# A two-layer decoder trunk: the loads of the modulation weights go from SyncE's DMA queue to GpSimd's, one background step ahead

## The chip, the cores and the metric

One core of one Trainium2 chip. The number that counts is the device time of one execution in microseconds, as the median of several runs.

## What is computed

Two decoder layers on 512 tokens of width 1024, in float32. In each layer the input is normalized and modulated, mixed by attention (a dilated attention with three head groups in layer 0, a forgetting attention in layer 1), added back through a gate, normalized and modulated again, and sent through 16 experts of which each token uses two. The six modulation rows of a layer come from one vector c:

```
ada_in = jax.nn.silu(c)
mod = (ada_in @ w_ada[i] + b_ada[i]).reshape(b, 6, d)
sh_m, sc_m, g_m = mod[:, 0, None, :], mod[:, 1, None, :], mod[:, 2, None, :]
sh_f, sc_f, g_f = mod[:, 3, None, :], mod[:, 4, None, :], mod[:, 5, None, :]
hm = rmsnorm(x, norm_mix[i]) * (1 + sc_m) + sh_m
...
x = x + g_m * y
hf = rmsnorm(x, norm_ffn[i]) * (1 + sc_f) + sh_f
x = x + g_f * hierarchical_moe(hf, ...)
```

Here `w_ada[i]` is 1024 x 6144, so that each of the six rows needs a 1024 x 1024 block of weights, 4 MB.

## The kernel before, in words

Matrix products run on TensorE as three float32r products of a high and a low part (`part`, L289). Weights arrive as tiles of 128 x 1024 floats through `Stream` (L78): `fetch` starts a load on SyncE's queue (L114), and `split` makes the high part on ScalarE (L150) and the low part on VectorE (L151).

The attention of layer 0 (`mixer_a`, L634) runs over four quarters of the heads. In each, a generator of main steps (`project`, L493) does projections, and `weave` (L225) puts steps of the attention of the quarter before between them. In every second main step `weave` also advances the first generator in a list of background jobs by one step. There are ten such jobs (`background`, L322): each makes one modulation row that is needed later, with `ada` (L382). The first two rows of layer 0 were made at the start (`begin`).

A job of `ada` clears an accumulator on GpSimd (L387) and puts the bias row into it (L388, on GpSimd's DMA queue). Then come eight steps, and in each it takes a tile of 512 KB, loads one eighth of the weights into it (L391, on SyncE's queue) and adds that tile, times one column of silu(c), to the accumulator on VectorE (L392, a scalar_tensor_tensor, STT below). In three of the jobs the fifth step also loads a row of norm weights (L394, SyncE's queue). After the eighth step ScalarE makes the high part (L397), VectorE the low part (L398), and three steps later four matmuls with a column of ones add up the partitions (L404, L407). The row is scaled (L411) or copied (L413) and written to memory by ScalarE's queue (L414).

The tiles of the weight stream and of the jobs share one pool tag, "raw", with four buffers. The stream holds at most three of them in this stage (L108), and a job takes one at a time.

The text of the program does not fix the order on an engine. A scheduler in the tile framework orders the instructions of each engine when the kernel is built, by priorities and a model of durations of its own, gives out the buffers and sets the waits. On the chip each engine and each DMA queue then goes through its list in that order, and an instruction that waits holds up all that stand behind it on the same engine.

Of the kernel before, what the change touches and what calls it, by code (L numbers as in the profile page):

```python
# [8 lines left out]
F32 = mybir.dt.float32  # L9
# [8 lines left out]
P = 128  # L18
D = 1024
S = 512  # L20
KT = D // P
# [154 lines left out]
class Trunk:  # L176
# [205 lines left out]
    def ada(self, layer, j, norm, put):  # L382

        nc, i = self.nc, self.i
        acc = self.w.tile([P, D], F32, name="acc", tag="acc", bufs=1)
        row = self.nrow
        nc.gpsimd.memset(acc, 0.0)  # L387
        nc.gpsimd.dma_start(out=acc[0:1, :], in_=i["b_ada"][layer:layer + 1, j * D:(j + 1) * D])  # L388
        for kt in range(KT):
            raw = self.w.tile([P, 1024], F32, name="ada", tag="raw", bufs=4)  # L390
            nc.sync.dma_start(out=raw, in_=i["w_ada"][layer, kt * P:(kt + 1) * P, j * D:(j + 1) * D])  # L391
            nc.vector.scalar_tensor_tensor(acc, raw, self.csil[:, kt:kt + 1], acc, op0=OP.mult, op1=OP.add)  # L392
            if norm is not None and kt == KT // 2:
                nc.sync.dma_start(out=row, in_=self.bcast(norm, D, 1))  # L394
            yield
        hi, lo = self.w.tile([P, 1024], F32R, name="ada", tag="raw", bufs=4), self.nlo
        nc.scalar.activation(hi, acc, AF.Copy)  # L397
        nc.vector.tensor_tensor(lo, acc, hi.bitcast(F32), op=OP.subtract)  # L398
        for _ in range(3):
            yield  # L400
        ts = [self.bank("s")[0:1, :], self.bank("s")[0:1, :]]
        for h in range(2):
            cs = slice(h * 512, (h + 1) * 512)
            nc.tensor.matmul(ts[h], lhsT=self.one, rhs=hi[:, cs], start=True, stop=False)  # L404
        for h in range(2):
            cs = slice(h * 512, (h + 1) * 512)
            nc.tensor.matmul(ts[h], lhsT=self.one, rhs=lo[:, cs], start=False, stop=True)  # L407
        for h in range(2):
            cs = slice(h * 512, (h + 1) * 512)
            if norm is not None:  # L410
                nc.vector.scalar_tensor_tensor(row[:, cs], ts[h], 1.0, row[:, cs], op0=OP.add, op1=OP.mult)  # L411
            else:
                nc.scalar.activation(row[:, cs], ts[h], AF.Copy)  # L413
        nc.scalar.dma_start(out=put, in_=row)  # L414
        if (layer, j) == (0, 2):
            self.g_m = self.load_row(layer, 2)
# [986 lines left out]
```

## Time and profile before

| what | value |
|---|---|
| median of 3 runs | 1437.47 us (1434.62 to 1438.4) |
| the profiled execution | 1427.06 us, span 1425.3 us |
| mean granted TensorE clock | 0.966 |
| PE busy (matmul) | 1311.6 us, 92% |
| DVE busy | 967.4 us, 68% |
| ACT busy | 652.4 us, 46% |
| POOL busy | 121.0 us, 8% |
| SyncE's DMA queue (q1) | 227.86 MB, 48.9% of 16 engines' time |
| GpSimd's DMA queue (q0) | 16.85 MB, 5.0% |

PE is TensorE, DVE VectorE, ACT ScalarE, POOL GpSimd, and SP SyncE, which only starts transfers; SPq is its queue. "Idle before" of a group is the time in which its engine did nothing just ahead of these instructions, with what ended most of it. The jobs of `ada` lie between 50 and 560 us; what the tables call "50 to 560" is this stage.

### The profile page before, as it was taken

Reading aid. Unit: us, or ns where it says so; the run is one execution under the profiler, and the core shown is the slowest. Engines: PE = TensorE matmul, PEld = TensorE weight load, DVE = VectorE, ACT = ScalarE, POOL = GpSimd, SP = SyncE. Lnnn points to the kernel's source line nnn. Section 1 sums busy time; section 2 is a strip of 40 time slices with the busy share of each in tenths; the row PEclk is TensorE's granted clock in tenths of the full one; section 3 lists DMA queues with packets and bytes.
Section 4 is the critical chain, followed back from the end, with each engine's and each line's share of the span. In section 5 each row is a group of like instructions: output and inputs, shape, how many; then the busy total and the mean of one; then the engine's idle time right before and its main releaser. Section 6 shows DMA issues by size and latency. Waiting matters only on the chain. (4 is left out here: it accounts for less than half of the span.)

```text
span 1425.3 us, 20009 instructions
## 1 busy us (share of the span) xinstructions
PE 1311.6 (92%) x7017; PEld 1068.2 (75%) x7017; DVE 967.4 (68%) x1913; ACT 652.4 (46%) x1356; POOL 121.0 (8%) x120
## 2 busy tenths in 40 slices
PE   5899999999998999989979998499999999699995
PEld 4787989888996899878756665268988978566662
DVE  6875776676677676655677775486767854877772
ACT  6433544344435444443355554354554542365560
POOL 0000000000000000000032221000000000223221
PEclk9899999999999999989979999799999999899998
DMA  9465445643554445264789997413321465799981
GB/s 360 138 207 179 153 156 162 202 141 120 169 191 151 161 148 164 82 218 149 254 268 313 294 295 233 148 50 95 112 65 62 134 202 191 258 288 303 302 278 22
DMA packets 187156, 264.14 MB, mean 185 GB/s; under 512 B 23065, under 2 KB 148697, under 8 KB 187047
## 3 DMA queue, kind: packets, MB, share of 16 engines
q1 hardware_dynamic: 160742, 227.86, 48.9%
q0 software_dynamic: 8576, 16.85, 5.0%
q10 hardware_dynamic: 17728, 18.05, 4.3%
q8 instruction: 59, 0.97, 0.3%
q14 instruction: 51, 0.41, 0.1%
HBM read 249.85 MB, written 25.43 MB: 193 GB/s over the span
## 5 line engine op out<-in xcount | busy, mean ns | idle before, releaser
L293 PE MATMUL ps_pj<-hi,h 128*128 128x512 f32 (+1 forms) x1016 | 390.6, 393 | 9.6 <-ACT h L453 5.0
L294 PE MATMUL ps_pj<-lo,h 128*128 128x512 f32 (+1 forms) x1016 | 371.9, 374 | 0.0
L296 PE MATMUL ps_pj<-hi,h 128*128 128x512 f32 (+1 forms) x1016 | 290.0, 374 | 0.0
L293 PEld LDWEIGHTS ps_pj<-hi,h 128*128 128x128 f32 x1016 | 238.6, 235 | 32.7 <-ACT h L453 7.1
L294 PEld LDWEIGHTS ps_pj<-lo,h 128*128 128x128 f32 x1016 | 240.3, 237 | 14.4 <-issue 0.8
L296 PEld LDWEIGHTS ps_pj<-hi,h 128*128 128x128 f32 x1016 | 211.5, 235 | 20.0 <-issue 1.1
L150 ACT ACTIVATE hi<-raw 128x1024 fp32r<-128x1024 f32 x126 | 132.4, 1052 | 130.3 <-PE ps_pj L296 70.7
L151 DVE TENSOR_TENSOR lo<-raw,hi 128x1024 fp32r<-128x1024 f32 x126 | 151.8, 1213 | 48.1 <-ACT hi L150 46.1
L392 DVE SCALAR_TENSOR_TENSOR acc<-ada,csil,acc 128x1024 f32<-128x1024 f32 x80 | 102.6, 1283 | 69.0 <-DMA ada<-in_w_ada 68.8
L293 PE MATMUL ps_pj<-hi,xh 128*112 128x512 f32 x256 | 104.9, 410 | 2.2 <-ACT xh L453 2.2
L294 PE MATMUL ps_pj<-lo,xh 128*112 128x512 f32 x256 | 104.2, 407 | 0.0
L296 PE MATMUL ps_pj<-hi,xl 128*112 128x512 f32 x256 | 80.8, 397 | 0.0
L453 ACT ACTIVATE xh<-ps_t 128x448 fp32r<-128x448 f32 x64 | 31.8, 542 | 81.8 <-PE ps_t L448 75.7
L1235 DVE SCALAR_TENSOR_TENSOR y<-ps_s,r_ws,g_f 112x512 f32<-112x512 f32 x64 | 47.8, 748 | 28.5 <-PE ps_s L1234 28.5
L462 DVE TENSOR_REDUCE qss<-sq 128x8 f32<-128x512 f32 x64 | 43.7, 682 | 31.5 <-ACT sq L460 30.8
L460 ACT ACTIVATE sq<-ps_pj 128x512 f32<-128x512 f32 x63 | 37.1, 589 | 57.7 <-PE ps_pj L296 50.9
L151 DVE TENSOR_TENSOR lo<-h,hi 128x1024 fp32r<-128x1024 f32 x42 | 51.1, 1223 | 15.4 <-ACT hi L150 14.6
L720 PEld LDWEIGHTS ps_o<-vr,pt 128*128 128x128 f32 x480 | 58.6, 193 | 1.4
L720 PE MATMUL ps_o<-vr,pt 128*128 128x64 f32 x480 | 57.8, 272 | 0.0
L293 PEld LDWEIGHTS ps_pj<-hi,xh 128*112 128x112 f32 x256 | 45.5, 178 | 15.4 <-ACT xh L453 3.1
L296 PEld LDWEIGHTS ps_pj<-hi,xl 128*112 128x112 f32 x256 | 44.9, 176 | 15.6 <-DVE xl L454 0.6
L927 ACT ACTIVATE nl<-nl,mn 128x128 f32<-128x128 f32 (+1 forms) x64 | 35.7, 559 | 40.6 <-DVE mn L925 40.1
(280 smaller groups left out, 2176.8 us busy)
## 6 DMA issues: line engine op xcount, KB each, us to landing
ada<-in_w_ada SPq DMA_DIRECT2D x85, 512.0 KB
raw<-in_a_w_in SPq DMA_DIRECT2D x128, 256.0 KB
h<-in_w_gate SPq DMA_DIRECT2D x42, 256.0 KB
h<-in_w_up SPq DMA_DIRECT2D x42, 256.0 KB
mix<-in_w_gate SPq DMA_DIRECT2D x37, 256.0 KB
mix<-in_w_up SPq DMA_DIRECT2D x37, 256.0 KB
raw<-in_w_down SPq DMA_DIRECT2D x18, 512.0 KB
h<-in_w_down SPq DMA_DIRECT2D x18, 512.0 KB
```

What stands on the lines that cost most here:

```text
L150: t.act = nc.scalar.activation(h, r, AF.Copy)
L151: nc.vector.tensor_tensor(l, r, h.bitcast(F32), op=OP.subtract)
L293: nc.tensor.matmul(out, lhsT=hi, rhs=wh, start=first and n == 0, stop=False)
L294: nc.tensor.matmul(out, lhsT=hi, rhs=wl, start=False, stop=False)
L296: nc.tensor.matmul(out, lhsT=lo, rhs=wh, start=False, stop=last and n == len(terms) - 1)
L392: nc.vector.scalar_tensor_tensor(acc, raw, self.csil[:, kt:kt + 1], acc, op0=OP.mult, op1=OP.add)
L453: self.nc.scalar.activation(hv, tv, AF.Copy)
L460: nc.scalar.activation(sq, ps, AF.Square)
L462: nc.vector.tensor_reduce(ss, sq.rearrange("p (h d) -> p h d", d=HD), axis=AX.X, op=OP.add)
L720: nc.tensor.matmul(held["o"][:, at:at + HD], lhsT=pt[:, a * P:(a + 1) * P], rhs=v, start=(m == 0), stop=(m == len(terms) - 1))
L927: nc.scalar.activation(pr[:, sl], pr[:, sl], AF.Exp, scale=-1.0, bias=mn, accum_out=held["d"][:, h * 4 + b:h * 4 + b + 1])
L1235: nc.vector.scalar_tensor_tensor(y[:, cs], yp, m["ws"][0:CAP, e:e + 1], m["g_f"][0:CAP, cs], op0=OP.mult, op1=OP.mult)
```

## The change

The loads of `ada` go to GpSimd's queue, and the load of the next eighth is written directly behind the STT of the one before, with a step of its own for the first load. A job has 13 steps where it had 12 (130 of the 140 that the stage's main steps give). The three norm rows go to ScalarE's queue.

```
         nc.gpsimd.dma_start(out=acc[0:1, :], in_=i["b_ada"][layer:layer + 1, j * D:(j + 1) * D])
+
+        def load(kt):
+            raw = self.w.tile([P, 1024], F32, name="ada", tag="raw", bufs=4)
+            nc.gpsimd.dma_start(out=raw, in_=i["w_ada"][layer, kt * P:(kt + 1) * P, j * D:(j + 1) * D])
+            return raw
+
+        raw = load(0)
+        yield
         for kt in range(KT):
-            raw = self.w.tile([P, 1024], F32, name="ada", tag="raw", bufs=4)
-            nc.sync.dma_start(out=raw, in_=i["w_ada"][layer, kt * P:(kt + 1) * P, j * D:(j + 1) * D])
             nc.vector.scalar_tensor_tensor(acc, raw, self.csil[:, kt:kt + 1], acc, op0=OP.mult, op1=OP.add)
+            if kt + 1 < KT:
+                raw = load(kt + 1)
             if norm is not None and kt == KT // 2:
-                nc.sync.dma_start(out=row, in_=self.bcast(norm, D, 1))
+                nc.scalar.dma_start(out=row, in_=self.bcast(norm, D, 1))
             yield
```

The scheduler answers with another order on every engine in this stage. In the new file lines behind L394 carry a number that is 10 higher (L404 becomes L414), the load L391 is L392 and the STT L392 is L400.

On PE, at the end of the fifth job, before (`ada` is the high part, `nlo` the low part, `qn` a normalized query and key block, `ps_pj` the bank of a projection):

```order
L293 MATMUL ps_pj<-hi,h 128x512
L294 MATMUL ps_pj<-lo,h 128x512
L296 MATMUL ps_pj<-hi,h 128x512 x2
L655 MATMUL ps_t<-J,qn 128x128 [waits DVE_49,Activation_49]
L656 MATMUL ps_t<-ident,qn 128x128
L655 MATMUL ps_t<-J,qn 128x128
L404 MATMUL ps_s<-ada,one 1x512 [waits Activation_49]
L404 MATMUL ps_s<-ada,one 1x512
L656 MATMUL ps_t<-ident,qn 128x128
```

and at the same place of the program after the change:

```order
L665 MATMUL ps_t<-J,qn 128x128
L666 MATMUL ps_t<-ident,qn 128x128
L296 MATMUL ps_pj<-hi,h 128x256 x2
L414 MATMUL ps_s<-ada,one 1x512 [waits DVE_49,PE_49]
L417 MATMUL ps_s<-nlo,one 1x512
L414 MATMUL ps_s<-ada,one 1x512 [waits DVE_49,PE_49]
L417 MATMUL ps_s<-nlo,one 1x512
```

The four matmuls now stand together and later, in the value projection, and the first of them no longer waits for ScalarE.

On SyncE's queue, behind the first quarter's loads of the near attention's result (`op`), before (`raw` are tiles of the weight stream):

```order
L765 DMA op<-near_d 128x264 x2
L391 DMA ada<-in_w_ada 128x1024 x5
L114 DMA raw<-in_a_w_in 128x4x256
L114 DMA raw<-in_a_w_in 128x2x256 x2
L391 DMA ada<-in_w_ada 128x1024
L114 DMA raw<-in_a_w_in 128x2x256 x4
L391 DMA ada<-in_w_ada 128x1024 x2
L394 DMA nrow<-in_norm_ffn 1x1024
L391 DMA ada<-in_w_ada 128x1024
```

and at the same place after:

```order
L775 DMA op<-near_d 128x264 x4
L114 DMA raw<-in_a_w_in 128x2x256 x6
L114 DMA raw<-in_a_w_in 128x4x256 x2
L114 DMA raw<-in_a_w_in 128x2x256 x26
L772 DMA near_d<-ox 128x264 x4
```

No job load stands between the weight loads any more, up to the next quarter's stores of `near_d`. On POOL the job loads now stand between the memsets, the bias rows and the merges of the near attention (L787, now L797); from the fifth job to the seventh:

```order
L387 MEMSET acc 128x1024
L388 DMA acc<-in_b_ada 1x16x64
L392 DMA ada<-in_w_ada 128x1024 x8
L387 MEMSET acc 128x1024
L388 DMA acc<-in_b_ada 1x16x64
L392 DMA ada<-in_w_ada 128x1024 x6
L797 TENSOR_TENSOR op<-op,mg_3656 128x4x256
L392 DMA ada<-in_w_ada 128x1024 x2
```

Before, POOL had no load of weights; now its order decides when these start, and a merge stands between the last two loads of the sixth job and the six ahead of them.

Behind the attention stage of layer 0 the order of the engines is the same as before.

## Rows read from the trace of the kernel before

**Rows 1.** Granted clock and busy time by stretch (busy us, in brackets instructions begun), attention stage of layer 0.
```profile
core 0: us, PE busy (x) PEld busy (x) DVE busy (x) ACT busy (x) POOL busy (x), PEclk, DMA share, GB/s
...
130.00:140.00 10.00, 7.71 (x39) 5.73 (x38) 6.35 (x14) 3.97 (x11) 0.00 (x0) 1.00 0.53 168
...
280.00:290.00 10.00, 5.98 (x24) 3.56 (x23) 7.46 (x19) 4.63 (x13) 0.00 (x0) 0.83 0.47 146
...
430.00:440.00 10.00, 5.83 (x27) 3.56 (x25) 7.55 (x18) 4.58 (x13) 0.00 (x0) 1.00 0.54 174
440.00:450.00 10.00, 9.89 (x56) 7.49 (x57) 5.40 (x14) 4.57 (x15) 1.47 (x2) 0.83 0.25 77
...
sum 510.00, PE 491.84 PEld 445.53 DVE 347.21 ACT 220.81 POOL 18.30; mean PE 9.64 PEld 8.74 DVE 6.81 ACT 4.33 POOL 0.36
```

**Rows 2.** The waits of PE, 50 to 560 us: us in total, times, longest.
```profile
PE ps_s L404 <- ACT ada L397: 10.8, 6, 3.1
...
PE ps_t L700 <- ACT nl L691: 2.4, 3, 0.8
PE ps_t L655 <- DVE qn L468: 1.8, 3, 1.1
PE ps_t L655 <- DVE rs_t L215: 1.6, 1, 1.6
PE ps_s L407 <- DVE nlo L398: 1.2, 3, 0.4
```

**Rows 3.** Timeline, end of the fifth job: start us, us, instruction, [idle before].
```profile
281.35 1.28 DVE L392 SCALAR_TENSOR_TENSOR acc<-ada,csil,acc 128x1024 f32<-128x1024 f32 x1
...
282.66 0.34 SPq L391 DMA_DIRECT2D ada<-in_w_ada  x1
...
286.95 1.28 DVE L392 SCALAR_TENSOR_TENSOR acc<-ada,csil,acc 128x1024 f32<-128x1024 f32 x1 [1.37 <-DMA ada<-in_w_ada]
...
288.27 1.06 ACT L397 ACTIVATE ada<-acc 128x1024 fp32r<-128x1024 f32 x1 [3.52 <-DVE acc L392]
...
289.38 0.63 PE L404 MATMUL ps_s<-ada,one 128*1 128x512 f32 x2 [2.28 <-ACT ada L397]
```

**Rows 4.** Groups of instructions by line, 50 to 560 us.
```profile
L392 DVE SCALAR_TENSOR_TENSOR acc<-ada,csil,acc 128x1024 f32<-128x1024 f32 x80 | 102.6, 1283 | 69.0 <-DMA ada<-in_w_ada 68.8
L151 DVE TENSOR_TENSOR lo<-raw,hi 128x1024 fp32r<-128x1024 f32 x62 | 75.2, 1222 | 17.6 <-ACT hi L150 16.1 <-DMA ada<-in_w_ada 1.0
```

**Rows 5.** The waits of DVE, 50 to 560 us.
```profile
DVE acc L392 <- DMA ada<-in_w_ada: 68.8, 49, 3.8
DVE qss L462 <- ACT sq L460: 24.3, 21, 2.2
DVE lo L151 <- ACT hi L150: 16.1, 19, 1.8
DVE rs_t L215 <- ACT rs_y L214: 14.1, 19, 1.8
```

**Rows 6.** The waits of SyncE's DMA queue, 50 to 560 us.
```profile
SPq L394 <- DMA mods<-nrow: 4.7, 2, 3.7
```

**Rows 7.** Tile ada, all instructions: count, min/median/max ns, first and last start.
```profile
L391 SPq DMA_DIRECT2D ada<-in_w_ada x80: 327/340/393, 52.8 to 539.6; - x80
```

**Rows 8.** GpSimd by line and shape, whole span.
```profile
L1196 POOL DMA_INDIRECT xr<-hf_d,r_ii x32 | 37.7, 1178 | 46.6 <-PE ps_t L448 34.5 <-issue 6.7 <-DVE r_wt L1161 5.1
...
L388 POOL DMA_DIRECT2D acc<-in_b_ada x10 | 5.0, 495 | 2.9 <-POOL acc L387 2.9
```

**Rows 9.** Timeline, POOL and DVE, at the first gathers of layer 0.
```profile
719.52 1.22 DVE L151 TENSOR_TENSOR lo<-mix,hi 128x1024 fp32r<-128x1024 f32 x1
...
719.82 1.84 POOL L1196 DMA_INDIRECT xr<-hf_d,r_ii  x1 [2.53 <-DVE r_wt L1161]
```

**Rows 10.** Timeline, PE, two matmuls in full flow.
```profile
109.94 0.40 PE L294 MATMUL ps_pj<-lo,h 128*128 128x512 f32 x1
110.18 0.40 PE L293 MATMUL ps_pj<-hi,h 128*128 128x512 f32 x1
```

## Prediction

> **What bounds the kernel now.** I read the page first: PE is 92% busy over the span, DVE 68%, POOL 8%. The change touches only the stage from 50 to 560 us, so I cut that stage into pieces of 10 us. It is TensorE's stage: PE is busy 491.84 of 510 us, DVE 347.21, POOL 18.30, and the 18.2 us in which PE did nothing lie in a few pieces, such as 2.3 us at 130 to 140, 4.0 us at 280 to 290 and 4.2 us at 430 to 440 [rows 1]. Two of the pieces have a granted clock of 0.83 in place of 1.00, one of them the slice with the 4.0 us gap, the other right behind the 4.2 us gap [rows 1]. So nothing can be won here beyond some 18 us of waits and about 3.4 us of clock (two times 10 us times 0.17); a faster load that PE never waited for is worth nothing.
>
> Next, who PE waited for. The largest item is L404, the matmul at the end of a background job, with 10.8 us in 6 waits, and L407 behind it with 1.2; the rest is transposes, 2.4, 1.8 and 1.6 us [rows 2]. No wait for weights of the projections is on that list, so that the weight loads on SyncE's queue, though they stand behind job loads, were in time for PE. One such end of a job in the timeline shows the chain [rows 3]: the seventh STT starts at 281.35 and ends some 1.28 us later; the eighth load is issued at 282.66, because its buffer is the one that this STT has just read; its STT starts at 286.95, 4.29 us after the issue; ScalarE's split starts at 288.27, and PE goes on at 289.38 after 2.28 us of nothing. The buffer, not the text of the program, sets when a load starts.
>
> DVE pays more than PE: the 80 STTs waited 68.8 us for their loads, 49 times [rows 4, 5]. DVE is idle 510 - 347.2 = 163 us in the stage, so 94 us of it for other reasons, of which 30 us are round trips through ScalarE (L151 16.1, L215 14.1) [rows 5]. PE felt little of that: its waits behind DVE and ScalarE work other than the job ends are 2.4 + 1.8 + 1.6 = 5.8 us [rows 2], 8% of 68.8.
>
> **The change, part by part.** *The fetch one step ahead.* The order of the built programs says which instruction frees the buffer of each load. I added up the DVE work that stands between that instruction and the STT, with the durations of the line groups (1.28 us for an STT, 1.22 for L151 [rows 4], and so on): 3.2 us on average over the 80 loads before, 3.4 after. The fetch ahead is hardly one: the four shared buffers are still handed on at the last moment. Its worth is about 0.25 us per load, for DVE.
>
> *The place of the final matmuls.* The extra step and the new order move L404 back. For each job I take PE's work from the last point at which DVE had to wait for PE to L404, with 0.24 us per 512-column matmul [rows 10], less DVE's work from the same point through the eighth STT. Before, this margin is 3.2, 2.0, 1.1, 5.1, 2.1, 1.1, 5.1, 2.1, 1.1 and 5.1 us for jobs one to ten: six jobs have 2.1 or less, and there were six waits. After, it is 3.2, 3.8, 4.6, 6.9, 7.4, 8.3, 6.4, 12.5, 9.9 and 4.1: all where no job waited before. I count 10 of the 12 us of L404 and L407 as gained, and 2 as left for jobs one to three and ten, since loads will come later (next item). If the cover is thinner than this, the 12 come back in part.
>
> *The queue.* All 80 loads leave SyncE's queue, where one takes 0.34 us to issue [rows 7]; GpSimd has to make their descriptors. The trace has no load of this shape on POOL. From below: the bias row's DMA takes 0.495 us there; the nearest row in size is the gather of 112 rows, 1.18 us [rows 8]; from above, a gather that started beside a low-part subtraction on DVE, 1.84 us [rows 9]. Against 0.34 that is 0.15, 0.84 or 1.5 us later per load. I take 0.84, for the size. POOL has room: 80 x 1.18 = 94 us on top of 18.3 in 510. Net of the 0.25 the STTs see loads 0.6 us later, 80 x 0.6 = 47 us more for DVE to wait. DVE's other idle time less the round trips, 94 - 30 = 64 us, covers that, but not everywhere: at 8% PE would feel 4 us. I take 5, and keep 0 and 12 (a quarter) as ends.
>
> Of descriptors made by GpSimd the Trainium skill (DMA: Bandwidth & Descriptors, Latency and other measured facts) gives a first byte after about 1 us, against about 0.6 for the hardware queues. By that a load would be 0.4 us later, less than the gather's row says, and the sum would be some 3 us better; no run here shows it yet.
>
> *SyncE's queue* loses 80 loads and the waits for their buffers. PE waited for no weight, so I cost this at nothing; it helps ScalarE and DVE to be early.
>
> *Norm rows.* Each must wait until the row before has been written out; on SyncE that was 4.7 us in 2 waits, up to 3.7 [rows 6]. On ScalarE such a wait holds up the work behind it; ScalarE is busy 221 of 510 us [rows 1]. Between 0 and 4.7, I take 1 us.
>
> *The clock.* The slow pieces lie at the two longest gaps; without them up to 3.4 us come back. The 1.6 us of transposes in the slice at 280 us may stay, so I take 1.5.
>
> Sum: -10 - 1.5 + 5 + 1 = **-5.5 us**. On the profiled execution's 1427.06 us that makes 1421.6; that execution was 10 us faster than the median shown, and I set the same difference against the median: 1437.5 - 5.5 = **1432 us**. A measurement of this kernel can tell about 0.3%, 4.3 us, from no change.
>
> **The rivals.** *A wash.* The loads are bound to their buffers as before, DVE's longer waits give PE some 12 us of new stalls, and the 12 us of the job ends are only half won: -6 - 1.5 + 12 + 1, or with the low end of the queue a little less. It gives 1437 within 4 us. For it: the lead of 3.2 to 3.4 us. Against it: the margins, all above 3, and PE's deafness to DVE's waits so far.
>
> *DVE becomes the bound, and it is slower.* Place: the 80 STTs. If loads come on average 1.2 us later than now, DVE waits 80 x (1.2 - 0.25) = 76 us more against 64 us of cover; 12 us go straight to PE, 5 as above, 1 for the norm rows, and of the job ends' 12 only 6 are won: +12 us, **1450 us**. It decides from about 64 / 80 + 0.25 = 1.05 us on. With 1.5 us for every load it would be 100 - 64 = 36 in place of 12, some 1474. For it: two-input operations on DVE stretched a gather from 1.18 to 1.84 us [rows 9], and this stage is full of them, 142 STTs and subtractions [rows 4]. Against it: the bias DMAs, also plain copies, took 0.495 us on average in the same stage [rows 8], and a plain load need not read a tile of indices as the gather does. This is a rule of the Trainium skill too (SBUF — State Buffer, SBUF: two separate sides): GpSimd cannot write descriptors while a DVE operation that uses both ports holds the pair they share. The page names two-input DVE operations as blocking only a GpSimd operation that reads SBUF, and the gather's row agrees with that; whether plain loads are spared, no row here shows at this size.
>
> *The gain is larger.* Loads as short as the bias row's (0.15 us later, less than the 0.25 of lead), all 12 us and 3.4 of clock: -15.4, 1422. It is the low end of the forecast's own range.
>
> **How the numbers follow.** The forecast (faster, 1422 to 1433) 0.50; the wash (1433 to 1441) 0.26; slower 0.24, of which about half lies above 1450. The range that leaves out no more than 2 in 10 goes from 1420 (the best case less 2 us, the scatter of the runs shown) to 1450. Faster 0.50, same 0.26, slower 0.24; the forecast's own range is 1422 to 1433.
>
> **What would show it.** Right: waits of PE at L414 of 2 us or less in total; no slice with a clock of 0.83 in this stage; PE idle in the stage near 13 us; plain loads on POOL about 1 us each; waits of DVE for `ada` near 110 us. If these DVE waits pass some 130 us and PE waits at transposes and low parts, the slower rival holds. If POOL's loads take 1.5 us or more beside two-input operations, the port is the cause. If L414 still waits 6 us or more, the margins were wrong. The prediction fails as a whole if time moves in a stage behind 560 us, where the order is unchanged.

## The result, and the profile after

The changed kernel takes 1454.78 us (median of 4 runs, 1451.2 to 1458.71) against 1436.59 us of the kernel before in the same comparison: a ratio of 1.0128, interval 1.0096 to 1.0159, so 18 us slower. The prediction was 1432 us, within 1420 to 1450.

The profiled execution of the changed kernel took 1458.71 us, that of the kernel before 1427.06: the one lies 4 us above its median, the other 10 us below. Differences between these two profiles are therefore some 13 us larger than those between the medians; a second profile of the change below (1452.53 us) helps to size its parts.

Where the time went is read best at landmarks. VectorE's large product in the merge of a quarter (L788, now L798) runs once per quarter; the third falls where the jobs were nearly done, the fourth lies behind the stage. From the timelines, before and then after:

```profile
561.03 2.95 DVE L788 TENSOR_TENSOR big<-big,mg 128x1024 f32<-128x1024 f32 x1
...
671.73 2.94 DVE L788 TENSOR_TENSOR big<-big,mg 128x1024 f32<-128x1024 f32 x1
```

```profile
573.01 2.95 DVE L798 TENSOR_TENSOR big<-big,mg 128x1024 f32<-128x1024 f32 x1
...
700.11 2.95 DVE L798 TENSOR_TENSOR big<-big,mg 128x1024 f32<-128x1024 f32 x1
```

So 12.0 us were lost up to the third merge and 16.4 more between the third and the fourth, by this landmark of VectorE; TensorE's own landmarks, shown with e13 below, divide the same 28 us into 17.1 and 11.5. From there to the end of the profiled execution it is 3.2 us more (31.6 in all), which is within what executions differ by.

The stage in the changed kernel, granted clock and busy time by stretch (columns as in [rows 1]):

```profile
50.00:560.00 510.00, 480.36 (x2611) 432.75 (x2612) 326.88 (x691) 211.99 (x524) 58.33 (x95) 0.97 0.49 152
...
260.00:270.00 10.00, 7.78 (x29) 6.15 (x29) 7.22 (x17) 3.36 (x8) 4.92 (x4) 0.83 0.25 72
310.00:320.00 10.00, 5.89 (x35) 4.55 (x34) 8.44 (x16) 6.26 (x14) 1.46 (x2) 0.83 0.53 156
430.00:440.00 10.00, 6.73 (x23) 4.45 (x23) 6.99 (x6) 4.68 (x7) 1.45 (x2) 0.83 0.47 149
...
560.00:590.00 30.00, 29.82 (x130) 28.69 (x129) 18.39 (x33) 10.97 (x21) 4.12 (x6) 1.00 0.48 151
590.00:600.00 10.00, 4.24 (x17) 3.11 (x17) 6.93 (x6) 0.57 (x1) 1.55 (x3) 0.94 0.77 263
600.00:610.00 10.00, 8.51 (x34) 5.67 (x35) 3.86 (x7) 4.18 (x9) 0.00 (x0) 0.71 0.65 215
```

TensorE does nothing for 510 - 480.36 = 29.6 us of the stage, against 18.2 before [rows 1]. The granted clock is lower in more slices, each of them at a gap or right behind one (the stage's first slice, 0.72 before and 0.69 now, lies behind gaps ahead of the stage in both kernels). Summed over the 51 slices of 10 us, 1 less the granted clock is worth 15.0 us, against 6.2 before. Gaps and clock together are 20 us up (11.4 and 8.8; in the second profile of the change 10.8 and 5.9). Further back, 590 to 610 us, stands a gap of 5.8 us with a clock of 0.71 behind it.

Who TensorE waited for in the stage (us in total, times, longest):

```profile
PE ps_t L665 <- DVE qn L478: 8.0, 6, 3.0
PE ps_t L710 <- DVE kt L670: 6.7, 3, 4.1
PE ps_s L414 <- ACT ada L407: 5.0, 3, 3.1
PE ps_t L710 <- ACT pt L205: 3.7, 3, 1.6
...
PE ps_t L665 <- DVE rs_t L215: 2.3, 1, 2.3
PE ps_s L417 <- DVE nlo L408: 1.3, 2, 0.7
```

The ends of jobs, 12 us before [rows 2], cost 6.3 now, without the tenth, whose end has moved behind this window. But the transposes that wait for VectorE (`qn`, `kt`), and for `pt` behind them, went from 1.8 us [rows 2] to 18.4. The longest of these waits in the timeline:

```profile
307.69 1.29 DVE L400 SCALAR_TENSOR_TENSOR acc<-ada,csil,acc 128x1024 f32<-128x1024 f32 x1 [2.24 <-DMA ada<-in_w_ada]
...
313.39 1.28 DVE L400 SCALAR_TENSOR_TENSOR acc<-ada,csil,acc 128x1024 f32<-128x1024 f32 x1 [1.25 <-DMA ada<-in_w_ada]
314.66 0.47 DVE L670 TENSOR_SCALAR kt<-ps_t,gains 128x256 f32<-128x256 f32 x1
...
315.19 0.78 PE L710 MATMUL ps_t<-ident,nl 128*128 128x128 f32 x4 [4.11 <-DVE kt L670]
```

VectorE stands at two STTs whose loads have not come, 2.24 and 1.25 us; `kt` stands behind them in its list, and TensorE waits for `kt`. Over the stage VectorE's wait for the loads went from 68.8 us [rows 5] to 100.8:

```profile
DVE acc L400 <- DMA ada<-in_w_ada: 100.8, 62, 4.4
```

The loads themselves, tile `ada` (duration on GpSimd in ns, min/median/max, and first and last start in us), and the page's time from issue to landing:

```profile
L392 POOL DMA_DIRECT2D ada<-in_w_ada x80: 527/530/582, 53.8 to 592.2; - x80
```

```profile
ada<-in_w_ada POOLq DMA_DIRECT2D x80, 512.0 KB, 4.3
```

A load takes GpSimd 0.53 us in every case, near the bias row's 0.495 [rows 8] and far from the gather's 1.18.

### The profile page after: what moved, and what is told of

The parts are those of the page before. It is cut to its first block, busy times and chain, and to the rows that moved or that the text cites. A ratio compares the mean times of both kernels' runs of the same rounds, so it can differ in the third digit from the quotient of the medians.

```text
span 1456.9 us, 20094 instructions
## 1 busy us (share of the span) xinstructions
PE 1325.5 (91%) x7017; PEld 1075.6 (74%) x7017; DVE 963.1 (66%) x1913; ACT 650.5 (45%) x1356; POOL 165.2 (11%) x200
## 3 DMA queue, kind: packets, MB, share of 16 engines
q0 software_dynamic: 20096, 58.80, 14.2%
## 5 line engine op out<-in xcount | busy, mean ns | idle before, releaser
L294 PEld LDWEIGHTS ps_pj<-lo,h 128*128 128x128 f32 x1016 | 240.8, 237 | 16.4 <-DVE lo L151 1.5
L296 PEld LDWEIGHTS ps_pj<-hi,h 128*128 128x128 f32 x1016 | 212.8, 236 | 20.4 <-issue 1.3
L400 DVE SCALAR_TENSOR_TENSOR acc<-ada,csil,acc 128x1024 f32<-128x1024 f32 x80 | 102.7, 1284 | 115.0 <-DMA ada<-in_w_ada 114.6
L392 POOL DMA_DIRECT2D ada<-in_w_ada x80 | 42.7, 534 | 438.0 <-DVE acc L400 192.4
L151 DVE TENSOR_TENSOR lo<-h,hi 128x1024 fp32r<-128x1024 f32 x42 | 51.1, 1222 | 15.5 <-ACT hi L150 14.7
```

The costliest lines, as they stand in the source:

```text
L151: nc.vector.tensor_tensor(l, r, h.bitcast(F32), op=OP.subtract)
L294: nc.tensor.matmul(out, lhsT=hi, rhs=wl, start=False, stop=False)
L296: nc.tensor.matmul(out, lhsT=lo, rhs=wh, start=False, stop=last and n == len(terms) - 1)
L392: nc.gpsimd.dma_start(out=raw, in_=i["w_ada"][layer, kt * P:(kt + 1) * P, j * D:(j + 1) * D])
```

## The experiments

Three explanations stood at the start; a fourth, **GpSimd's order** (what costs is that the loads stand behind other work in GpSimd's list), came with e5. **Queue**, later called late loads: a load reaches VectorE later through GpSimd's queue. **Place**: the thirteenth step of a job shifts the last job to where its end holds up the weights of the value projection. **Prefetch**: the load that is written ahead takes buffers from the weight stream. The table has every run; the ratio is to the kernel before on the same chip. Idle is 510 us less PE's busy time from 50 to 560 us, clock the sum of (1 - granted clock) x 10 us over the slices of that stage, merges the starts of VectorE's large product in the third and fourth quarter (from the timelines). The one profile of the kernel before (1427.06 us) lies some 4 us below the medians of 1431.0 to 1431.6 us that this kernel had beside e1 to e16, so delays against it may be too large by as much, in all rows alike.

| kernel | queue | steps | ahead | stream's buffers | ratio (interval) | idle | clock | 3rd merge | 4th less 3rd |
|---|---|---|---|---|---|---|---|---|---|
| before | SyncE | 12 | no | 3 | 1 | 18.2 | 6.2 | 561.0 | 110.7 |
| the change | GpSimd | 13 | yes | 3 | 1.0128 (1.0096 to 1.0159) | 29.6 | 15.0 | 573.0 | 127.1 |
| e9, the same | GpSimd | 13 | yes | 3 | 1.0152 (1.0114 to 1.0190) | 29.0 | 12.1 | 568.4 | 125.7 |
| e13 | GpSimd | 13 | no | 3 | 1.0174 (1.0152 to 1.0197) | 30.8 | 14.8 | 572.5 | 123.4 |
| e10 | GpSimd | 12, 13 | yes | 3 | 1.0123 (1.0088 to 1.0158) | 29.6 | 10.9 | 571.7 | 120.2 |
| e2 | GpSimd | 12 | no | 3 | 1.0119 (1.0077 to 1.0161) | 25.7 | 14.9 | 571.4 | 111.5 |
| e14, the same | GpSimd | 12 | no | 3 | 1.0092 (1.0067 to 1.0117) | 29.1 | 14.3 | 573.2 | 115.1 |
| e1 | GpSimd | 12 | yes | 3 | 1.0046 (1.0024 to 1.0068) | 27.7 | 14.2 | 574.5 | 109.9 |
| e15, the same | GpSimd | 12 | yes | 3 | 1.0050 (1.0025 to 1.0074) | 25.3 | 14.7 | 571.1 | 109.1 |
| e5 | half and half | 12 | no | 3 | 1.0059 (1.0040 to 1.0077) | 24.8 | 11.0 | 566.3 | 115.5 |
| e3 | SyncE | 13 | yes | 3 | 1.0018 (0.9993 to 1.0044) | 17.9 | 12.3 | 559.7 | 117.8 |
| e4 | SyncE | 13 | no | 3 | 1.0007 (0.9988 to 1.0026) | 14.9 | 5.7 | 550.4 | 120.5 |
| e11, norm rows only | SyncE | 12 | no | 3 | 1.0028 (1.0002 to 1.0054) | 20.4 | 8.0 | 566.0 | 109.6 |
| e6 | GpSimd | 13 | yes | 2 | 0.9908 (0.9875 to 0.9941) | 10.0 | 5.3 | 542.6 | 117.9 |
| e7 | GpSimd | 12 | yes | 2 | 0.9949 (0.9928 to 0.9970) | 16.0 | 5.6 | 553.7 | 110.5 |
| e8 | SyncE | 12 | no | 2 | 0.9917 (0.9885 to 0.9950) | 10.4 | 4.5 | 545.4 | 112.7 |
| e16 | GpSimd | 12 | no | 2 | 0.9898 (0.9867 to 0.9928) | 10.7 | 8.3 | 546.3 | 113.4 |
| e12 | SyncE | 13 | yes | 2 | 0.9935 (0.9912 to 0.9958) | 10.8 | 2.4 | 544.2 | 113.4 |

Where the table says "yes" under ahead, the norm rows are on ScalarE's queue too, as in the change.

### Which part costs: e1 to e4

**e1**, the change without its additional step:

```
         raw = load(0)
-        yield
         for kt in range(KT):
```

> The change without its additional step: a job has 12 steps as before, the loads stay on GpSimd's queue, each behind the STT of the one before. PE, ACT and DVE times of the ends of jobs move back to where they stood before the change. Theory 'place' (the 13th step shifts the last job into the end of the stage, where its serial chain of load and STT, some 5.6 us per step, holds up the last weights of the value projection: a PE gap of 6.4 us and a granted clock of 0.5 for 7 us behind it, 17 us of delay between 570 and 600 us): about 1437 us, within 5, no PE wait over 4 us between 540 and 620 us. Theory 'queue' (a load lands later from GpSimd's queue): 1450 us or more. Theory 'prefetch' (the earlier request takes buffers from the weight stream): 1450 or more.

**e2**, the queue alone, in the kernel before:

```
-            nc.sync.dma_start(out=raw, in_=i["w_ada"][...])
+            nc.gpsimd.dma_start(out=raw, in_=i["w_ada"][...])
```

> The kernel before with one edit: the 80 loads of the jobs on GpSimd's queue; 12 steps, no fetch ahead, norm rows on SyncE's queue. Theory 'place': 1437 us within 5. Theory 'queue': 1450 us or more, VectorE's waits for these loads near 100 us in the stage against 68.8 before, and TensorE's waits behind VectorE up by 10 us or more. Theory 'prefetch': 1437 within 5.

**e3**, the change with the loads back on SyncE's queue (that line the other way round):

> The change with one edit undone: the loads back on SyncE's queue; 13 steps, each load behind the STT of the one before, norm rows on ScalarE's queue. Theory 'place': 1450 to 1458 us, with a PE gap of 5 us or more near 590 to 600 us at the end of the tenth job. Theory 'queue': 1437 within 5. Theory 'prefetch': 1450 to 1458.

**e4**, the additional step alone, in the kernel before:

```
         nc.gpsimd.dma_start(out=acc[0:1, :], in_=i["b_ada"][...])
+        yield
         for kt in range(KT):
```

> The kernel before with one edit: an empty step at the start of every job (13 steps); loads on SyncE's queue, none ahead. Theory 'place': 1450 to 1458 us, the tenth job ends near 600 us in place of 547 and PE has its gap there. Theory 'queue' and theory 'prefetch': 1437 within 5.

Measured: 1.0046, 1.0119, 1.0018 and 1.0007. The two kernels on SyncE's queue are not slower by anything that can be measured, the two on GpSimd's are. e1's 1438.5 us lies where its expectation put theory 'place', but the kernel before took 1431.5 us beside it, so that the ratio has to decide; e2's own signs came a little short (1448 us, 88 us of waits). Place alone and prefetch alone both fall as explanations of the whole; the queue is the condition. The landmarks say when: e1 and e2 are 13.4 and 10.4 us late at the third merge, as the change is (12.0), and lose little or nothing from there to the fourth.

What the queue does to one link of the chain shows in e2 at the place of [rows 3], the end of the fifth job:

```profile
281.30 2.61 DVE L392 SCALAR_TENSOR_TENSOR acc<-ada,csil,acc 128x1024 f32<-128x1024 f32 x2 [1.08 <-DMA ada<-in_w_ada]
...
282.88 0.53 POOL L391 DMA_DIRECT2D ada<-in_w_ada  x1 [4.86 <-DVE acc L392]
...
287.25 1.28 DVE L392 SCALAR_TENSOR_TENSOR acc<-ada,csil,acc 128x1024 f32<-128x1024 f32 x1
...
288.83 0.53 POOL L391 DMA_DIRECT2D ada<-in_w_ada  x1 [5.42 <-DVE acc L392]
...
293.00 1.28 DVE L392 SCALAR_TENSOR_TENSOR acc<-ada,csil,acc 128x1024 f32<-128x1024 f32 x1 [1.17 <-DMA ada<-in_w_ada]
...
294.31 1.06 ACT L397 ACTIVATE ada<-acc 128x1024 fp32r<-128x1024 f32 x1 [3.32 <-DVE acc L392]
```

The STT at 287.25 ends at 288.53 and frees the buffer; the load starts at 288.83, 0.30 us later. On SyncE's queue that was 0.03 us (281.35 + 1.28 to 282.66, [rows 3]). Over all jobs the median of this interval is 0.03 us before and 0.30 in e2. From its start to an STT that waited for it, the shortest load took 3.30 us before and 3.55 in e2. The medians of this time, over the loads that were waited for, do not show the difference (4.30 and 4.21 us); between e4 and e13, which differ by the queue alone too, they do (3.85 and 4.09). So each link of load, STT, next load is an estimated 0.27 + 0.25 = 0.5 us longer.

TensorE in e2: the stage as a whole, two of its stretches with a gap, and the waits at the ends of jobs with the largest other one:

```profile
50.00:560.00 510.00, 484.30 (x2620) 434.81 (x2621) 336.54 (x698) 214.73 (x526) 60.60 (x102) 0.97 0.50 158
```

```profile
190.00:200.00 10.00, 6.86 (x26) 5.03 (x26) 5.74 (x17) 4.78 (x14) 1.91 (x3) 0.83 0.30 95
...
500.00:510.00 10.00, 7.57 (x27) 5.93 (x27) 6.80 (x19) 4.01 (x13) 0.66 (x2) 0.83 0.28 85
```

```profile
PE ps_s L404 <- ACT ada L397: 14.9, 7, 3.5
PE ps_t L700 <- ACT nl L691: 5.0, 3, 2.5
...
PE ps_s L407 <- DVE nlo L398: 2.3, 5, 0.6
```

VectorE waited 87.8 us for these loads in e2, 19 more than before. TensorE's gaps grew by 7.5 us (25.7 against 18.2), 5.2 of them at the ends of jobs (14.9 + 2.3 against 12.0), and the clock took 8.7 us more (14.9 against 6.2): most of the gaps now bring a slice of 0.83 with them. This profile is the fastest of e2's five executions (1438.72 us, median 1448.38); in that of e14, the same kernel at its median, gaps and clock are 10.9 and 8.1 us up.

The waits alone do not decide. In e3 VectorE waits 84.5 us for these loads, 16 more than before, and TensorE's gaps do not grow (17.9 us): the place of a wait counts, and not the sum.

### The dose, and the norm rows: e5 and e11

**e5**, the odd eighths on GpSimd's queue:

```
+            (nc.gpsimd if kt % 2 else nc.sync).dma_start(out=raw, in_=i["w_ada"][...])
```

> The kernel before with the odd eighths of every job (40 of 80 loads) on GpSimd's queue and the even ones on SyncE's. Theory 'late loads' (on GpSimd's queue a load starts 0.26 us later after its buffer is free and lands 0.25 us later after its start, so each link of the chain load, STT, next load is 0.5 us longer, and TensorE pays in gaps and in clock): half the price of moving all 80, a ratio of 1.004 to 1.008 to the kernel before. Theory 'GpSimd's order' (what costs is that loads stand behind merges, memsets and each other in one list): under 1.003, since SyncE's list takes half of the loads out of it.

1.0059: half of the loads, between half and two thirds of the price of e2 and e14. This speaks for a price per load, and against GpSimd's order, for which under 1.003 was expected.

**e11**, the norm rows alone on ScalarE's queue:

> The kernel before with the three norm rows on ScalarE's queue and nothing else. Prediction: some 1 us slower at most; every theory here: a ratio of 0.998 to 1.002.

1.0028, 0.3 to 8 us: a little more than forecast, and small beside the queue.

### A buffer to spare: e6, e7, e8, e16, e12

The test of late loads is to hide the delay. The stream is held to two of the four shared buffers, so that a job has two and the next load need not wait for the STT of this one:

```
-        elif self.held["raw"] < (4 if self.moe else 3):
+        elif self.held["raw"] < (4 if self.moe else 2):
```

**e6** is the change with this edit, **e7** the change without its step and with it, **e8** the kernel before with it, **e16** e2 with it, **e12** e3 with it.

> The change with the weight stream held to two buffers of the shared tag in place of three in the attention stages, so that a job has two and the load of the next eighth can really start before the STT of this one ends. Theory 'late loads': the 0.5 us per load is hidden, VectorE waits under 60 us for these loads in the stage (114.6 in the changed kernel), and the ratio to the kernel before is 1.000 to 1.005 with what the place of the tenth job costs. Theory 'GpSimd's order': stays at 1.010 or above. Against both: with two buffers the weights of the projections may be late, TensorE then waits at matmuls of the projections for low parts or ScalarE waits for weights over 60 us.

> The change without its additional step (12 steps) and with the weight stream held to two shared buffers. Theory 'late loads': the delay is hidden and no tenth job stands at the end: a ratio of 0.995 to 1.000 to the kernel before, against 1.0046 with three buffers. Theory 'GpSimd's order': 1.005 or above.

> The kernel before with the weight stream held to two shared buffers; loads on SyncE's queue, 12 steps. What the second buffer of a job does without GpSimd's queue: theory 'late loads': VectorE's 68.8 us of waits for these loads fall under 40 and the ratio is 0.990 to 0.998. If the weights of the projections are late instead, above 1.003.

> The kernel before with the loads on GpSimd's queue and the weight stream held to two shared buffers, nothing else. Theory 'late loads': the queue's price is hidden by the second buffer, within 0.004 of the 0.9917 that the same kernel has on SyncE's queue. If GpSimd's list costs by its order: 1.000 or above.

> The change with the loads back on SyncE's queue and the weight stream held to two shared buffers: 13 steps, a fetch ahead that has its buffer, norm rows on ScalarE's queue. Theory 'late loads' (with a buffer to spare the queue no longer matters): the ratio is within 0.004 of the 0.991 that the same kernel has with GpSimd's queue. If the queue still mattered: 0.985 or under.

All five are faster than the kernel before, 0.9898 to 0.9949. With the second buffer the queue costs nothing: e16 (GpSimd) 0.9898 and e8 (SyncE) 0.9917, e6 (GpSimd) 0.9908 and e12 (SyncE) 0.9935. The same move that costs 1% with one buffer per job is free with two, and GpSimd's order, for which 1.000 or above was expected in e16, falls. The timelines show that the buffer does what it was added for: of the 79 loads that follow another one, 17 start before the STT of the one before has started in the kernel before, as many in the change with its load written ahead, 15 in e2, but 48 to 50 in e16, e8 and e6. VectorE's wait missed what e8 expected (63 us in place of under 40) and is 68.5 us in e16, no less than before, while TensorE's gaps fall to 10.4 and 10.7 us; e6 gained more than expected. The stage and TensorE's waits at the ends of jobs in e16:

```profile
50.00:560.00 510.00, 499.25 (x2734) 459.08 (x2734) 354.68 (x727) 224.34 (x545) 62.69 (x103) 0.98 0.53 167
```

```profile
PE ps_s L404 <- ACT ada L397: 4.0, 3, 2.9
PE ps_s L404 <- DVE st L689: 2.6, 2, 1.3
...
PE ps_s L407 <- DVE nlo L398: 0.6, 1, 0.6
```

These are the waits that the change was expected to shorten, 7.2 us in place of 12.0. e16, e6 and e8 beat both kernels and can't be told apart by their intervals (1416.4, 1420.0 and 1421.0 us beside 1431.0 to 1431.6 of the kernel before); e8 gets there by one digit in the kernel before.

### The end of the tenth job: e9, e10, e13

**e9** is the change once more; **e10** has the additional step in the first five jobs only (`if len(self.bg) > 5:` ahead of the `yield`); **e13** is e4 with the loads on GpSimd's queue.

> The change as it is, once more, for a second profile and a second ratio: 1.010 to 1.016 to the kernel before. Theory 'late loads and place': the same two parts as in the first profile, some 15 us of delay up to 560 us (gaps and clock) and some 10 us between 560 and 610 us, at the end of the tenth job.

> The change with the additional step in the first five jobs only (125 steps of the 140), so that the tenth job ends five steps sooner. Theory 'place' (the last job's end falls on the last weights of the value projection): the delay between 560 and 610 us is gone (under 3 us) and the ratio to the kernel before falls to 1.003 to 1.008, against 1.013 with ten such steps and 1.0046 with none. If the additional step costs in all jobs alike: 1.008 to 1.010, with the delay spread over the stage.

> The kernel before with two edits: an empty step at the start of every job (13 steps) and the loads on GpSimd's queue; none ahead, norm rows on SyncE's queue. If queue and place add up with nothing else: 1.010 to 1.016 like the change, 10 to 17 us of delay up to 560 us and 6 to 12 us more at the end of the tenth job. If the load written ahead is what makes the additional step dear: 1.004 to 1.008.

Between the third and the fourth merge a kernel with 12 steps takes 109.1 to 115.5 us, on either queue. With 13 steps and three buffers it takes 117.8 and 120.5 us on SyncE's queue, 123.4 to 127.1 on GpSimd's. That is the place: ten more steps move the matmuls at the end of the tenth job from 547 us to 601.

TensorE's own landmarks divide the loss more sharply than VectorE's merge: the last products of the attention weights with the values (`ps_o`) in the third quarter and the first ones in the fourth, before and after the change:

```profile
536.19 1.89 PE L720 MATMUL ps_o<-vr,pt 128*128 128x64 f32 x16
...
591.57 1.89 PE L720 MATMUL ps_o<-vr,pt 128*128 128x64 f32 x16
```

```profile
553.25 1.89 PE L730 MATMUL ps_o<-vr,pt 128*128 128x64 f32 x16
...
620.17 1.89 PE L730 MATMUL ps_o<-vr,pt 128*128 128x64 f32 x16
```

At the last matmul of the first group all eight kernels with every load on GpSimd's queue and three buffers are 12.6 to 17.1 us late, with e5's half of the loads it is 10.5, and on SyncE's queue -7.8 to 4.8. From there to the first matmul of the second group the kernels with 12 steps take 53.4 to 54.3 us on either queue; those with 13 steps and three buffers 61.7 and 62.8 on SyncE's queue and 65.3 to 66.1 on GpSimd's. So the change pays twice: 13 and 17 us in its two profiles for the queue (some 4 us of it perhaps the fast profile before), and 12.3 and 11.5 for the tenth job.

At the end of the tenth job the changed kernel shows (timeline, rows of VectorE, GpSimd, SyncE's queue, ScalarE and one of TensorE):

```profile
584.43 0.54 POOL L392 DMA_DIRECT2D ada<-in_w_ada  x1 [5.05 <-DVE acc L400]
...
588.38 1.28 DVE L400 SCALAR_TENSOR_TENSOR acc<-ada,csil,acc 128x1024 f32<-128x1024 f32 x1 [4.25 <-DMA ada<-in_w_ada]
...
589.58 3.49 DVE L151 TENSOR_TENSOR lo<-raw,hi 128x1024 fp32r<-128x1024 f32 x3
...
589.96 0.53 POOL L392 DMA_DIRECT2D ada<-in_w_ada  x1 [4.99 <-DVE acc L400]
...
592.23 0.53 POOL L392 DMA_DIRECT2D ada<-in_w_ada  x1 [0.60 <-DVE lo L151]
...
593.10 0.37 SPq L114 DMA_DIRECT2D raw<-in_a_w_in  x1
...
598.25 1.28 DVE L400 SCALAR_TENSOR_TENSOR acc<-ada,csil,acc 128x1024 f32<-128x1024 f32 x1 [1.44 <-DMA ada<-in_w_ada]
...
599.43 1.06 ACT L150 ACTIVATE hi<-raw 128x1024 fp32r<-128x1024 f32 x1 [11.95 <-DMA raw<-in_a_w_in]
...
600.40 1.04 ACT L407 ACTIVATE ada<-acc 128x1024 fp32r<-128x1024 f32 x1
...
601.49 1.01 PE L414 MATMUL ps_s<-ada,one 128*1 128x512 f32 x2 [6.40 <-ACT ada L407]
```

VectorE stands at an STT whose load is under way (4.25 us). Three low parts whose high parts ScalarE had finished by 586.5 us stand behind it in its list; their buffers come free late, so the job's last load starts at 592.23 only and reaches its STT 6.0 us later, and the stream's last load for the value projection starts at 593.10 and reaches ScalarE 11.95 us after its last work. TensorE has nothing for 6.4 us.

e10 missed: it was to fall to 1.003 to 1.008 and gave 1.0123; five steps less are not enough to clear the place (120.2 us from merge to merge, 60.1 between TensorE's landmarks). Nor does the place explain why the step costs nothing on SyncE's queue (1.0007) and about 0.8% on GpSimd's (e14 1.0092 and e13 1.0174). e4 is 10.7 us early at the third merge, so it gains from later ends of jobs what it loses at the tenth, while e13 is 11.5 us late, no better than e2 and e14. Why the gain of the step vanishes on GpSimd's queue was not isolated.

### Repeats: e14 and e15

> The kernel before with the loads on GpSimd's queue and nothing else, again. Theory 'late loads': the same price as with the load written ahead in the next run, since the buffer and not the text sets when a load starts: both between 1.004 and 1.012 and within 0.003 of each other.

> The change without its additional step, again: within 0.003 of the run before this one. If writing the load ahead does help on this queue, it stays 0.005 or more below it.

1.0092 and 1.0050, after 1.0119 and 1.0046: the expectation of equal times missed, and the other, 0.005 or more, is missed by a little. With both pairs the load written ahead does help by some 0.4 to 0.7% here, though it seldom starts earlier (19 of the 79 loads before the STT ahead, 15 and 16 in e2 and e14). The profiles do not place it: by TensorE's landmark in the third quarter e15 is 4.4 us ahead of e14, and e1 0.5 us behind e2. How the gain arises stays open.

## Why the prediction was wrong

- **The bound.** TensorE's stage, its gaps and the ends of jobs as their largest group: right. That a load's start is set by the buffer and not by the text: right, and the key to the rest, since a second buffer brings what the change was expected to bring.
- **The delay per load.** Taken as 0.84 us less 0.25 of lead, 0.6 net. GpSimd's 0.53 us per load is the row of the bias (0.15 over SyncE's queue), not that of the gather. A second delay that the prediction did not have, 0.27 us more from the freed buffer to the start, brings the link to an estimated 0.5 us. It stood in [rows 8], as 2.9 us of idle time ahead of the ten bias rows, 0.29 each. By luck the size was right, and VectorE's waits were too: forecast near 110, measured 100.8. The 0.25 us of lead does not show in the starts (17 of 79 loads ahead of the STT before them, in both kernels); writing the load ahead still gives 0.4 to 0.7%, by a way that stays open.
- **From VectorE's waits to TensorE: the step that failed.** The prediction let 64 us of VectorE's idle time cover them and took 5 us from a share of 8%. That share was an average of the kernel before, and it is no slope: e2 adds 19 us of waits on VectorE and TensorE's gaps grow by 7.5 us, 40%, while e3 adds 16 and they do not grow. In the change `qn`, `kt` and `pt` cost TensorE 18.4 us in place of 1.8. A waiting STT stands in VectorE's list ahead of `qn`, `kt` and the weights' low parts, and TensorE meets it wherever these have no slack, as at 315 and 595 us, whatever the idle time adds up to elsewhere.
- **The clock: the second mis-sized term, with the wrong sign.** -1.5 us was forecast; it cost 8.7 us in e2 and 8.8 in the change (5.9 in its second profile). In e2 the gaps at the ends of jobs grew longer, in the change new ones came at transposes, and the clock fell with them.
- **The ends of jobs.** -10 was forecast, 12.0 to 6.3 us is -5.7 in the stage; with the 6.4 us of the tenth job it is 12.7, and nothing was won. By the prediction's own sign (6 us or more at L414; 5.0 + 6.4 were measured) the margins were wrong: jobs four and seven, with 6.9 and 6.4 us counted, waited 1.6 and 3.1 us. That links longer by 0.5 us used the margins up is likely, and not shown job by job.
- **The tenth job.** Its margin of 4.1 us was taken as enough, and only TensorE's wait for the job was looked at. What stood behind its STTs on VectorE, the last low parts, and the buffers that these hold, was not. From the third to the fourth merge the change loses 16.4 and 15.0 us in its two profiles, by TensorE's own landmarks 11.5 and 12.3; the prediction had nothing there. This lies behind 560 us, where no time was to move, because the job itself has moved there.
- **SyncE's queue** without the loads gave nothing, as forecast. **Norm rows** 1 us forecast, 0.3 to 8 measured.
- **The rivals.** Slower, with VectorE's list as the place, is what happened; but its threshold (1.05 us per load) was derived from the same average cover and was twice too high, and its sign, over 130 us of waits on VectorE, did not come (100.8). The wash's sum was wrong in itself: -6 - 1.5 + 12 + 1 is +5.5, 1443 us, and not the 1433 to 1441 that it was given. The port as its cause fell: 80 loads took 527 to 582 ns, beside two-input operations or not. With this the rule of the Trainium skill (SBUF — State Buffer, SBUF: two separate sides), that two-input DVE operations block a GpSimd operation that reads SBUF, was not contradicted; it does not reach plain loads in these runs.
- The Trainium skill (DMA: Bandwidth & Descriptors, Latency and other measured facts) had a first byte 0.4 us later on GpSimd's path. The runs show 0.25 us from start to use and 0.27 ahead of the start, together a little more; the sum by it would have failed at the same step.

## What to carry to other kernels

Before a load is moved to another queue or written earlier, find what frees its buffer: if that is the reader of the load before, the chain is serial, the text hardly moves the start, and each added half microsecond comes back in every link, until a buffer is added (here one taken from the weight stream gave 0.8 to 1.0%). An average of idle time is no cover: follow what stands behind the waiting instruction in its engine's list, and count the clock with each new gap. When steps are added to background work, look where its last piece ends.

## What the runs showed of the hardware that was not expected

- A load of 512 KB takes GpSimd 0.53 us, 527 to 582 ns over 80 loads, less than half of a 112-row gather (1.18 us [rows 8]), and beside VectorE's two-input operations no longer.
- From the end of the instruction that frees the buffer to the start of the load it is 0.30 us on GpSimd (e2) and 0.03 us on SyncE's queue (before), as medians; no busy time shows the 0.30.
- In e2 slices of 10 us in which TensorE is idle for 3.1 us (at 190) and 2.4 us (at 500) have a granted clock of 0.83, while before one with 2.3 us (at 130) kept 1.00 [rows 1]. What the clock took beside the gaps that came was of their size: 8.7 and 7.5 us in e2, 8.1 and 10.9 in e14.
